# A planner inside a transformer kernel gets other estimates for POOL's pow, for each kind of matmul and for visits to half mode

## The chip, the cores and the metric

One Trainium2 chip (trn2); the kernel runs on one core. The time is device time of one execution in microseconds, and of several executions the median. A second, profiled execution gives the trace.

## The reference

Input is x of 256 tokens by 1024, all in float32. Five layers follow one another, each with a residual:

- **layer ab**: RMS norm, a projection to queries, keys and values, a sparse attention whose keys are picked by an index score (top 64 of 256), a forgetting attention beside it (8 heads of 64 each), an output projection
- **mlp**: RMS norm, 1024 to 4096, squared relu, 4096 to 1024
- **layer c**: RMS norm, a projection, an attention of 16 heads in three branches (compressed, selected, window) with gates, an output projection
- **mlp** again, then a last RMS norm
- **layer d**: differential attention, where each of 16 heads has two score maps of 64 columns each whose softmaxes are subtracted

```python
q = rms_norm(q.reshape(b, s, 16, 2, 64), q_norm_g) * 64 ** -0.5
k = rms_norm(k.reshape(b, s, 16, 2, 64), k_norm_g)
scores = einsum('bqhmd,bkhmd->bhmqk', q, k)
probs = softmax(scores + alibi_bias, axis=-1)
weights = probs[:, :, 0] - lam * probs[:, :, 1]
o = rms_norm(einsum('bhqk,bkhe->bqhe', weights, v), head_norm_g) * (1 - lam_0)
out = x + (o.reshape(b, s, 2048) * silu(z)) @ w_out
```

## The kernel before

**Staging.** All weights come from HBM once, in loads of 512 KB that one generator (`fetch`) issues in a fixed sequence on SP's queue. Each load is split into a high part, rounded to float32r (`round_off`, on ACT or VectorE), and a remainder (`remainder`, on VectorE). A product is a **triple** of matmuls into one PSUM bank (`mm3`): high by high, high by low, low by high. The 256 tokens are two tiles t = 0, 1 of 128. `proj` runs eight k-steps of such triples for both tiles into two banks and hands each finished bank to an evacuation; `out_proj` does the same for the four output banks. The two MLPs are the longest stretches: seven chunks, each with 96 matmuls of 256 columns (up) and 48 of 512 (down), after a first one.

**The order is made by a planner.** Nothing in the kernel's text fixes the order of instructions. Every stage is a generator, a strand, that yields one operation at a time or a wait for an event, a buffer or a time. `_Weaver.run` (line 217) simulates the engines: T is TensorE, A ACT, D VectorE, P POOL, Q SP's queue. At each step it takes the strand that can start first (ties by priority, then by age), emits its operation, and moves the engine's clock on by the operation's cost. `LAT` (line 157) is added where an operation's input comes from another engine. Where a strand offers a list of operations, one per engine, the one that ends first in the plan is taken. What is emitted is the program: each engine runs its instructions in exactly that order, and on the chip semaphores make it wait wherever an operand isn't there.

So an estimate does nothing to an instruction's own time. It decides what stands ahead of it on its engine. The costs come from two places: `_Engine.cost` (line 116) for ACT, VectorE and POOL, and `T` (line 325) for TensorE. The planner also keeps a count of TensorE's work for its clock (`clock`, line 180): where the count is low, it takes TensorE's costs double.

**POOL's pow.** A reciprocal square root is a `tensor_tensor` with `pow` and a constant of -0.5 on POOL (`rsqrt`, line 519), on one column (a row's norm), four (`drn`) or eight (`qrs`).

**The turn from one head group to the next in layer d.** `group` (line 1661) runs four projections per group (q, k, v, z), then spawns four heads whose attention is woven into the next group's projections. The evacuation of q and of k is `qk_ev` (line 1640): Square on ACT, a reduction `qss` on VectorE, a scalar step, the pow `qrs` on POOL, a scaling `n` on VectorE, then `transp4` (line 660): four transposes on TensorE and a copy back.

```python
yield act.activation(out=sq, in_=ps, func=AF.Square)
te = yield dve.tensor_reduce(out=ss, in_=heads(sq), axis=AX.X, op=ALU.add)
yield dve.tensor_scalar(out=ss, in0=ss, scalar1=rq[t], scalar2=EPS, op0=ALU.mult, op1=ALU.add)
rs = yield from rsqrt(ss, 8, "qrs")
te = yield dve.scalar_tensor_tensor(out=heads(q), in0=heads(ps), scalar=r[t], in1=rs..., op0=ALU.mult, op1=ALU.mult)
yield from transp4(q, dst[:, :, t * P:(t + 1) * P], gp, evs[t])
```

**Half mode.** Scores of heads of 64 columns are done two heads at a time (`scores2`, line 680): the operands of one head lie on partitions 0 to 63, of the other on 64 to 127, so each matmul uses half of the array's rows, and two run beside one another. One such operation, four float32 matmuls (recorded as eight), is a **visit**. They occur in the index of layer ab, in its two attentions, and in the heads of layer d.

**Ropes.** `rope_on` (line 633) rotates the first 16 columns of each head with four POOL operations: three products into `T` and one sum into `n`; a rope over eight heads has the widths 128, 64, 64 and 128.

The line of almost every operation in the trace is 113 (ACT, VectorE, POOL), 341 (matmuls) or 339 (transposes): these are the helpers that emit it. So rows are told apart by tiles: `wH` and `wL` are a weight's high part and remainder, `slot` the big buffers, `n` the 512-column buffers, `uH` and `uL` a layer's input, `E` a score map.

Of the kernel before, what the change touches and what calls it, by code (L numbers as in the profile page):

```python
# [10 lines left out]
F32 = mybir.dt.float32  # L11
F32R = mybir.dt.float32r
# [73 lines left out]
class _Op:  # L86
# [4 lines left out]
    def __init__(self, eng, cost, emit, bank=None, work=0.0):  # L91
        self.eng, self.cost, self.emit, self.bank, self.work = eng, cost, emit, bank, work


def _free(ap):
    n = 1
    for x in ap.shape[1:]:
        n *= x
    return n


class _Engine:
# [13 lines left out]
    def cost(self, name, a, kw):  # L116
        out = kw.get("out", a[0] if a else None)
        src = kw.get("in_", kw.get("in0", a[1] if len(a) > 1 and hasattr(a[1], "shape") else out))
        n = _free(out)
        if name in ("tensor_reduce", "max"):  # L120
            n = _free(src)
        ptr = sum(hasattr(kw.get(k), "shape") for k in ("scale", "bias", "scalar", "scalar1", "scalar2"))
        ps = src.space == PSUM
        if self.key == "A":
            return 1e-3 * (n / 1.2 + (52 if ps else 93) + 93 * (ptr + ("accum_out" in kw)))
        if self.key == "D":
            if name == "reciprocal":
                return 1e-3 * (69 + 6.25 * n)
            fast = name in ("tensor_copy", "tensor_scalar") and not ps
            return 1e-3 * (69 + n * (0.521 if fast else 1.042) + 62 * ptr)  # L130
        if name == "dma_start":
            return 1.04
        if kw.get("op") == ALU.pow:
            return 1e-3 * (300 + 165 * n)
        if name == "tensor_scalar":
            return 1e-3 * (260 + 3.35 * n)
        return 1e-3 * (147 + (3.1 if name == "tensor_copy" else 2.11) * n)
# [124 lines left out]
def tile_kernel(ctx: ExitStack, tc: tile.TileContext, I: dict, out: bass.AP):  # L262
# [23 lines left out]
    X0 = 2  # L286
    GAINW = 5.5
    HALF = 0
    T1W = 0
    LATE = 7  # L290
    OWN = 8
# [33 lines left out]
    def T(calls, beside=1):  # L325
        late = calls if callable(calls) else lambda: calls
        cost = work = 0.0
        for c in late():
            if len(c) == 3:
                cost += 0.109  # L330
                work += 0.053
            else:
                work += _free(c[0]) * (4 if c[1].dtype == F32 else 1) * c[1].shape[0] / 128 * 0.4167e-3
                cost += 0.003 + (4 * max(_free(c[0]), 128) if c[1].dtype == F32 else max(_free(c[0]), 256 if c[1].dtype == F32R else 128)) * 0.4167e-3

        def emit():
            for c in late():
                if len(c) == 3:
                    i = pe.transpose(c[0], c[1], ident[:c[2], :c[2]])  # L339
                else:  # L340
                    i = pe.matmul(c[0], lhsT=c[1], rhs=c[2], start=c[3], stop=c[4], skip_group_check=True)  # L341
            return i
        return _Op("T", cost / beside, emit, None, work)

    def events(n, m):
        return [[_Event() for _ in range(m)] for _ in range(n)]
# [123 lines left out]
    def setup():  # L470
        def across(dst, src):
            return pool.dma_start(out=dst, in_=src.partition_broadcast(P))

        yield pool.dma_start(out=grow[0:2, :], in_=I["a_kv_norm"][0].rearrange("(k p) -> k p", p=P))
        yield across(kidx_b, I["a_kidx_norm"][0])
        yield across(bforget_b, I["ab_b_forget"][0])
        early.set(W.end + 4.0)
        yield pool.dma_start(out=grow[2:18, :], in_=I["mlp_norm"].rearrange("l (k p) -> (l k) p", p=P))
        for r0, src in ((18, I["final_norm"]), (26, I["l0_norm_g_2"]), (34, I["l0_head_norm_g_2"])):
            n = src.shape[0] // P  # L480
            yield pool.dma_start(out=grow[r0:r0 + n, :], in_=src.rearrange("(k p) -> k p", p=P))
        for r0, src in ((35, I["l0_q_norm_g_2"]), (36, I["l0_k_norm_g_2"])):
            for j in range(2):
                yield pool.dma_start(out=grow[r0:r0 + 1, 64 * j:64 * j + 64], in_=src.rearrange("(k p) -> k p", k=1))
        yield ("at", W.end + GAINW)
        yield ("acq", "B")
        b = bank()
        yield T([tr(b[:, :NG], grow, NG)])
        te = yield dve.tensor_copy(gcol, b[:, :NG])
        W.give("B", te)  # L490
        gain.set(te + 0.2)
        yield dve.tensor_tensor(out=gfd, in0=gcol[:, G_F:G_F + 8], in1=gcol[:, G_D:G_D + 8], op=ALU.mult)
        yield across(bgate_b, I["c_b_gate"][0])


    def warm():
        yield ("acq", "B")
        b = bank()
        while W.now < WARM:
            yield T([mm(b[:, :256], warmth[:, :P], warmth, True, True)])  # L500
        W.give("B", W.end)

    def first_gain():
        yield ("at", 3.2)
        yield ("acq", "B")
        b = bank()
        yield T([tr(b[:, :NA], growA, NA)])
        te = yield dve.tensor_copy(gcolA, b[:, :NA])
        W.give("B", te)
        gainA.set(te + 0.1)  # L510
# [40 lines left out]
    def start_layer(gap, gev, hev, after, first=4, late=None):  # L551
        uev = [[_Event() for _ in range(8)] for _ in range(2)]
        for t in range(2):
            n = first if t == 0 else 4
            for k in range(0, 8, n):
                W.spawn(u_strand(t, k, n, gap, gev, hev, uev[t][k:k + n], late), t + 0.1 * k)
            W.spawn(after(t), 1.5)
        return uev
# [39 lines left out]
    def out_proj(lds, opnd, ev, finish, last=4, halves=False):  # L598
        nk = len(lds)
        pieces = [(t, c * 512, 512) for t in range(2) for c in range(2)]  # L600
        if halves:
            pieces[3:] = [(1, 512, S), (1, 512 + S, S)]
        yield ("acq", "B", len(pieces))
        acc = [bank()[:, :n] for _, _, n in pieces]

        def step(k, i):
            ld = lds[k]
            t, a, n = pieces[i]
            yield ("ev", ld.ready)
            yield ("ev", ev(k))  # L610
            lH, lL = opnd(k, t)
            w = slice(a, a + n)
            yield T(mm3(acc[i], lH, lL, ld.H[:, w], ld.L[:, w], k == 0, k == nk - 1))
            if i != 3 or not halves:
                ld.took()

        for k in range(nk - last):
            for i in range(len(pieces)):
                yield from step(k, i)
        for i, (t, a, n) in enumerate(pieces):  # L620
            for k in range(nk - last, nk):
                yield from step(k, i)
            W.spawn(finish(t, a // 512, acc[i], slice(a, a + n)), 0, W.end + 0.2)
# [292 lines left out]
    def norm_after(hin, r, rev, late=None):  # L916
        def after(t):
            for c in range(2):
                yield ("ev", hin[t][c])
            if late is not None:  # L920
                yield ("ev", late)
            ms = yield from mean_sq(h[:, t, :], D, "ms")
            r[t] = yield from rsqrt(ms, 1, "r")
            rev[t].set(W.end + 0.1)
        return after

    def layer_ab(pl, hin, hout):
        r, rev = [None, None], [_Event(), _Event()]
        aqiw = pl["aqi"]["ld"][LATE].ready
        uev = start_layer(gcolA[:, 0:8], gainA, hin, norm_after(hin, r, rev, aqiw), 2,  # L930
                          pl["aqi"]["ld"][T1W].rounded)
        yield None
# [637 lines left out]
    def layer_d(pl, hin):  # L1570
# [229 lines left out]

        yield from out_proj(pl["out"], opnd, lambda k: oev[k], fin, halves=bool(HALF))

# [52 lines left out]
```

## Time and profile before

| what | value |
| --- | --- |
| median of 3 runs | 924.11 us (922.16 to 925.39) |
| the profiled execution | 921.53 us |
| its span, first to last instruction | 919.4 us |
| mean granted TensorE clock | 0.998 |
| instructions | 14126 |
| TensorE matmuls | 5196 |
| VectorE, ACT, POOL busy | 586.6, 518.2, 106.4 us |
| DMA | 144.55 MB, mean 157 GB/s |

Times in the rows are microseconds from the span's start, unless a column says nanoseconds. A matmul's record lasts longer than its share, since matmuls overlap: what one costs is the distance from its start to the next start. `[0.71 <-DVE n L113]` means that the engine sat idle 0.71 us until VectorE had written n.

### The profile page before, as it was taken

How to read it: one execution, taken by the hardware profiler on the slowest of the kernel's cores; microseconds unless marked ns; L12 is line 12 of the kernel's file. 1: busy time of each engine (PE TensorE's matmuls, PEld its weight loads, DVE VectorE, ACT ScalarE, POOL GpSimd, SP SyncE). 2: the span in 40 equal slices, each digit the busy share in tenths (PEclk: the TensorE clock that was granted, in tenths of full speed). 3: DMA queues.
4: the chain of work that ended last, by engine and by line, in shares of the span. 5: the costliest groups of instructions: out<-in, count | busy, mean ns of one | idle time of the engine just before them, and what ended most of it. 6: DMA issues, size and time to landing. Idle time of an engine off the chain costs nothing.

```text
span 919.4 us, 14126 instructions
## 1 busy us (share of the span) xinstructions
PE 901.2 (98%) x5196; PEld 766.9 (83%) x5196; DVE 586.6 (64%) x1230; ACT 518.2 (56%) x1025; POOL 106.4 (12%) x149
## 2 busy tenths in 40 slices
PE   8999999999999999999999999999999999999998
PEld 6778888999999878888789999998877778777786
DVE  5688646544454457766654445444878878697781
ACT  5666858455544564787575544455637545274450
POOL 3520000000000051120000000000310503204000
PEclk9999999999999999999999999999999999999999
DMA  7756134655555474312236665655674545544431
GB/s 233 207 178 211 55 104 164 203 183 187 189 191 190 133 249 143 110 46 70 74 123 196 208 192 179 198 184 161 161 220 130 159 138 160 165 133 159 140 115 46
DMA packets 65124, 144.55 MB, mean 157 GB/s; under 512 B 7214, under 2 KB 9744, under 8 KB 65056
## 3 DMA queue, kind: packets, MB, share of 16 engines
q1 hardware_dynamic: 63632, 140.68, 48.0%
q0 software_dynamic: 1424, 2.98, 1.6%
q8 instruction: 41, 0.67, 0.3%
q14 instruction: 27, 0.22, 0.1%
HBM read 142.59 MB, written 1.05 MB: 156 GB/s over the span
## 4 chain that ended last, share of the span: by engine, by line
PE 86%; DVE 4%; POOL 4%; DMA 3%; ACT 1%; issue 1%; SPq 0%; POOLq 0%; DVEq 0%; ACTq 0%
PE bank L341 81%; PE bank L339 5%; POOL qrs L113 2%; DVE wL L113 2%; DVE n L113 1%; DMA h<-in_x_dram 1%; ACT wH L113 1%; DMA raw<-in_c_w_in_dram 1%; POOL T L113 1%; POOL drn L113 1%; DMA raw<-in_ab_w_in_dram 1%; DVE qss L113 0%; DMA raw<-in_l_w_in_dram 0%; ACT n L113 0%; DVE dss L113 0%
## 5 line engine op out<-in xcount | busy, mean ns | idle before, releaser
L113 DVE TENSOR_TENSOR wL<-raw,wH 128x1024 fp32r<-128x1024 f32 (+2 forms) x262 | 317.8, 1214 | 187.9 <-ACT wH L113 186.2
L113 ACT CAST wH<-raw 128x1024 fp32r<-128x1024 f32 (+2 forms) x226 | 234.8, 1041 | 225.4 <-PE bank L341 181.4
L341 PE MATMUL bank<-wH,slot 128*128 128x512 f32 (+1 forms) x784 | 258.3, 396 | 1.2 <-ACT slot L113 0.6
L341 PE MATMUL bank<-wH,uH 128*128 128x512 f32 (+2 forms) x448 | 182.8, 408 | 0.5 <-ACT uH L113 0.5
L341 PE MATMUL bank<-wH,uL 128*128 128x512 f32 (+2 forms) x448 | 174.9, 390 | 0.0
L341 PE MATMUL bank<-wL,uH 128*128 128x512 f32 (+2 forms) x448 | 174.6, 390 | 0.0
L341 PEld LDWEIGHTS bank<-wH,slot 128*128 128x128 f32 x784 | 147.2, 188 | 32.1 <-issue 1.7
L341 PE MATMUL bank<-wL,slot 128*128 128x512 f32 (+1 forms) x392 | 152.7, 390 | 0.0
L341 PE MATMUL bank<-uH,wL 128*128 128x256 f32 x448 | 127.4, 284 | 0.0
L341 PE MATMUL bank<-uL,wH 128*128 128x256 f32 x448 | 127.0, 284 | 0.0
L341 PE MATMUL bank<-uH,wH 128*128 128x256 f32 x448 | 126.1, 281 | 0.0
L341 PEld LDWEIGHTS bank<-wH,uH 128*128 128x128 f32 x448 | 85.1, 190 | 20.2 <-issue 2.3
L341 PEld LDWEIGHTS bank<-wH,uL 128*128 128x128 f32 x448 | 84.8, 189 | 18.7 <-DVE uL L113 0.4
L341 PEld LDWEIGHTS bank<-wL,uH 128*128 128x128 f32 x448 | 85.2, 190 | 15.0 <-DVE wL L113 0.2
L341 PEld LDWEIGHTS bank<-uH,wH 128*128 128x128 f32 x448 | 85.0, 190 | 0.6
L341 PEld LDWEIGHTS bank<-uL,wH 128*128 128x128 f32 x448 | 84.3, 188 | 0.6
L341 PEld LDWEIGHTS bank<-wL,slot 128*128 128x128 f32 x392 | 73.8, 188 | 13.0
L341 PEld LDWEIGHTS bank<-uH,wL 128*128 128x128 f32 x448 | 84.6, 189 | 0.0
L113 ACT ACTIVATE E<-E,nb 128x128 f32<-128x128 f32 (+1 forms) x160 | 70.8, 447 | 9.7 <-DVE nb L113 9.6
L113 POOL TENSOR_TENSOR qrs<-qss,neghalf 128x8 f32<-128x8 f32 x16 | 36.3, 2272 | 141.6 <-DVE dss L113 110.0
L341 PEld LDWEIGHTS bank<-slot,PT 128*128 128x128 f32 x384 | 48.7, 191 | 3.9 <-issue 0.7
L113 POOL TENSOR_TENSOR r<-ms,neghalf 128x1 f32<-128x1 f32 x6 | 4.0, 668 | 403.3 <-DVE ms L113 403.3
(206 smaller groups left out, 953.4 us busy)
## 6 DMA issues: line engine op xcount, KB each, us to landing
raw<-in_mlp_w_dram SPq DMA_DIRECT2D x128, 512.0 KB, 3.9
raw<-in_l_w_in_dram SPq DMA_DIRECT2D x64, 512.0 KB, 3.8
raw<-in_ab_w_in_dram SPq DMA_DIRECT2D x16, 512.0 KB, 4.1
raw<-in_l_w_out_dram SPq DMA_DIRECT2D x16, 512.0 KB, 3.4
raw<-in_c_w_in_dram SPq DMA_DIRECT2D x12, 512.0 KB, 4.0
raw<-in_ab_w_out_dram SPq DMA_DIRECT2D x8, 512.0 KB, 3.4
raw<-in_c_w_out_dram SPq DMA_DIRECT2D x8, 512.0 KB, 3.5
slot<-in_ab_w_in_dram SPq DMA_DIRECT2D x8, 256.0 KB, 6.2
```

The costliest lines, as they stand in the source:

```text
L113: return _Op(self.key, self.cost(name, a, kw), lambda: f(*a, **kw), bank[0] if bank else None)
L339: i = pe.transpose(c[0], c[1], ident[:c[2], :c[2]])
L341: i = pe.matmul(c[0], lhsT=c[1], rhs=c[2], start=c[3], stop=c[4], skip_group_check=True)
```

## The change

Four edits in the planner's estimates, none in an operation. In `_Engine.cost`, pow on n columns of POOL costs 0.380 us and 0.175 us a column below eight columns, 0.380 and 0.262 a column from eight on; before it was 0.300 and 0.165 a column. In `T`, a float32r matmul costs 0.0145 us and 0.4167 ns a column (at least 0.112), before 0.003 and the same a column (at least 256 columns). A float32 matmul costs twice 0.004 us and two columns' time a column (at least twice 0.112), before 0.003 and four columns' time (at least 128 columns). Other types keep their formula, with the least cost written as a time. The transposes' cost stays. A T operation that has a matmul on 64 partitions, or with 64 stationary columns, costs 0.4 us more (`SWITCH`), after its sum is divided by the number that run beside one another. The count of work for the clock stays as it was.

```diff
         if kw.get("op") == ALU.pow:
-            return 1e-3 * (300 + 165 * n)
+            return 1e-3 * (380 + (175 if n < 8 else 262) * n)
...
     HALF = 0
+    SWITCH = 0.4
...
         cost = work = 0.0
+        mode = False
         for c in late():
             if len(c) == 3:
                 cost += 0.109
                 work += 0.053
+                continue
+            n = _free(c[0])
+            work += n * (4 if c[1].dtype == F32 else 1) * c[1].shape[0] / 128 * 0.4167e-3
+            mode = mode or c[1].shape[0] == 64 or _free(c[1]) == 64
+            if c[1].dtype == F32:
+                cost += 2 * max(0.112, 0.004 + 2 * n * 0.4167e-3)
+            elif c[1].dtype == F32R:
+                cost += max(0.112, 0.0145 + n * 0.4167e-3)
             else:
-                work += _free(c[0]) * (4 if c[1].dtype == F32 else 1) * c[1].shape[0] / 128 * 0.4167e-3
-                cost += 0.003 + (4 * max(_free(c[0]), 128) if c[1].dtype == F32 else max(_free(c[0]), 256 if c[1].dtype == F32R else 128)) * 0.4167e-3
+                cost += max(0.056, 0.003 + n * 0.4167e-3)
+        cost = cost / beside + (SWITCH if mode else 0.0)
...
-        return _Op("T", cost / beside, emit, None, work)
+        return _Op("T", cost, emit, None, work)
```

## Rows read from the trace of the kernel before

**Rows 1.** The page, busy time of each engine (share of the span) and its instructions.
```profile
PE 901.2 (98%) x5196; PEld 766.9 (83%) x5196; DVE 586.6 (64%) x1230; ACT 518.2 (56%) x1025; POOL 106.4 (12%) x149
```
**Rows 2.** Busy time by stage: stage, length, each engine, clock, DMA share, GB/s.
```profile
317.00:350.00 33.00, 31.12 (x166) 26.89 (x165) 19.38 (x38) 22.56 (x48) 13.35 (x28) 0.95 0.68 212
...
424.00:465.00 41.00, 37.37 (x231) 30.38 (x229) 26.05 (x92) 26.34 (x83) 2.20 (x3) 1.00 0.19 66
...
713.00:736.00 23.00, 22.08 (x112) 17.86 (x112) 18.06 (x38) 11.50 (x16) 12.13 (x6) 1.00 0.53 156
```
**Rows 3.** The chain of waits: start, length, what; the second MLP and a turn.
```profile
479.16 158.87 PE bank L341 x1008
...
727.08 2.49 POOL qrs L113
...
730.62 2.49 POOL qrs L113
```
**Rows 4.** TensorE in order of time around one visit to half mode in layer d.
```profile
695.66 0.40 PE L341 MATMUL bank<-wH,uL 128*128 128x512 f32 x1
695.99 0.93 PE L341 MATMUL bank<-slot 64*128 64x128 f32 x8
696.84 0.50 PE L341 MATMUL bank<-wH,uH 128*128 128x512 f32 x1
697.18 0.39 PE L341 MATMUL bank<-wL,uH 128*128 128x512 f32 x1
```
**Rows 5.** POOL in order of time: a pow of one column, one of eight.
```profile
327.76 0.56 POOL L113 TENSOR_TENSOR r<-ms,neghalf 128x1 f32<-128x1 f32 x1 [3.64 <-DVE ms L113]
...
717.18 1.63 POOL L113 TENSOR_TENSOR qrs<-qss,neghalf 128x8 f32<-128x8 f32 x1
```
**Rows 6.** TensorE in order of time: the first group's transposes, and the first turn.
```profile
675.80 0.40 PE L341 MATMUL bank<-wH,uL 128*128 128x512 f32 x1
676.49 0.66 PE L339 MATMUL bank<-const,n 128*128 128x128 f32 x4 [0.29 <-DVE n L113]
...
720.54 1.03 PE L339 MATMUL bank<-const,n 128*128 128x128 f32 x8
...
724.55 0.48 PE L341 MATMUL bank<-wH,uH 128*128 128x512 f32 x1
...
729.29 0.40 PE L341 MATMUL bank<-wH,uL 128*128 128x512 f32 x1
730.40 0.66 PE L339 MATMUL bank<-const,n 128*128 128x128 f32 x4 [0.71 <-DVE n L113]
...
733.44 0.39 PE L341 MATMUL bank<-wH,uL 128*128 128x512 f32 x1
734.03 0.63 PE L339 MATMUL bank<-const,n 128*128 128x128 f32 x4 [0.21 <-DVE n L113]
```
**Rows 7.** VectorE in order of time: three scalings n at the first turn.
```profile
719.68 0.74 DVE L113 SCALAR_TENSOR_TENSOR n<-bank,rr,qrs 128x512 f32<-128x512 f32 x1
...
729.59 0.75 DVE L113 SCALAR_TENSOR_TENSOR n<-bank,rr,qrs 128x512 f32<-128x512 f32 x1 [0.94 <-POOL qrs L113]
...
733.13 0.75 DVE L113 SCALAR_TENSOR_TENSOR n<-bank,rr,qrs 128x512 f32<-128x512 f32 x1 [1.53 <-POOL qrs L113]
```
**Rows 8.** The chain of waits at layer C's start and at its end.
```profile
335.16 6.54 DMA raw<-in_c_w_in_dram
...
457.10 1.23 DVE wL L113
```
**Rows 9.** POOL's groups by line and shape: count, busy us, mean ns, idle before.
```profile
L113 POOL TENSOR_TENSOR T<-n,const 128x64 f32<-128x64 f32 x16 | 7.4, 481 | 0.0
L113 POOL TENSOR_TENSOR n<-T,T 128x128 f32<-128x128 f32 x8 | 5.6, 696 | 0.5
...
L113 POOL TENSOR_TENSOR T<-n,const 128x128 f32<-128x128 f32 x8 | 4.1, 515 | 24.5 <-ACT n L113 22.2 <-PE bank L341 2.2
```
**Rows 10.** TensorE's waits: for what, us in total, times, longest.
```profile
PE bank L339 <- POOL n L113: 0.7, 1, 0.7
```

## The prediction

> **What bounds the kernel now.** I read the page first: TensorE is busy for 98% of a 919.4 us span, and the next engine for 64% [rows 1]. The reader is to see that only TensorE time counts, and that an edit which adds and removes no instruction can win only what TensorE loses between instructions. Where that is stands in the busy time by stage [rows 2]: layer C's start has 31.12 of 33.00 with a granted clock of 0.95, its end 37.37 of 41.00, and in the last layer a turn from one head group to the next has 22.08 of 23.00; there are three turns, alike. The chain of waits [rows 3] says what a turn waits for: a pow of 2.49 us on POOL and then a second one of 2.49. Its piece of 1008 matmuls, in an MLP, gives the true price of a stretch with nothing to win, 158.87 us.
>
> **The estimates against the rows.** The change edits only what the planner believes, so each belief is set beside its row.
>
> Matmuls: those 1008 are seven chunks with 96 of 256 columns (672) and 48 of 512 (336) each. By the old formula (0.003 us plus 0.4167 ns a column) they cost 672 x 0.1097 + 336 x 0.2163 = 146.4 us, by the new one (0.0145 us plus the same) 672 x 0.1212 + 336 x 0.2278 = 158.0. The chip took 158.87 [rows 3]. So the old plan has TensorE 8.5% too fast, the new one 0.6%. A triple of 512 columns (the planner's unit) goes from 0.649 to 0.683; the chip's is 0.70 (successive starts 0.23 apart, [rows 4]). The Trainium skill, page "TensorE: Matmul & The Clock Gate", section "Back-to-back issue gap", gives N / 2.4 + 2.5 ns, 216 ns at 512 columns. By that rule the old figure is right and the new one 5% too long; dependents would come later in the plan than they need, the lost slack below would be nil, and the sum would be -3.6 instead of -3.1 us. The trace disagrees with the rule: 0.23 us [rows 4].
>
> Visits to half mode: the last triple ahead of a visit begins its third matmul at 695.66, so the visit can begin at 695.89; the next matmul starts at 696.84 and takes 0.34 to its successor instead of 0.23 [rows 4]. That is 0.95 + 0.11 = 1.06 us. The planner had (2 x 0.2163 + 2 x 0.4297) / 2 = 0.646, and will have (2 x 0.224 + 2 x 0.4347) / 2 + 0.4 = 1.059. By the code there are 28 visits (four of the index, four in each of the two attentions of the first layer, 16 in the last), so 28 x 0.41 = 11.6 us of TensorE time become known to the plan. The visits themselves get no cheaper: 0, and nothing hides them.
>
> Pow: eight columns go from 1.620 to 2.476, four from 0.960 to 1.080, one from 0.465 to 0.555. The rows have 2.49 [rows 3] and 1.63 [rows 5] for eight, and 0.56 for one [rows 5].
>
> **What moves, and the sum.** At a turn the planner's chain from a projection's last matmul to the transposes of its result is 0.2 + Square 0.479 + 0.13 + reduction 0.602 + 0.127 + scalar step 0.135 + 0.155 + pow 1.620 + 0.06 + scaling 0.664 + 0.2 = 4.37 us, or 6.7 triples of 0.649, so seven are laid ahead of the transposes. The trace has exactly these seven (21 matmuls from 724.55), and TensorE then waits: its last matmul starts at 729.29 and the transposes at 730.40, 1.11 later where 0.23 would do, a loss of 0.88 us; at the second pair 733.44 to 734.03, a loss of 0.36 [rows 6]. The other two turns repeat both losses, and the first group has one of 0.46 at 675.80 [rows 6]. With the new figures the chain is 5.23 us, or 7.65 triples of 0.683: eight. One more triple is 0.70 us of TensorE work inside the 0.88. The second pair lies behind two pows, so it moves by 1.7 us in the plan, over two triples, and its 0.36 goes whole. Gain: 3 x (0.70 + 0.36) + 0.46 = **3.6 us**; of 0.88, 0.18 stays, because VectorE's weight remainders stand in the chain too. Late next is VectorE, where the scaling is queued among them: it starts at 729.59 only, after 0.94 us of waiting for POOL [rows 7]. The triples that move forward need their weights then; these are in hand, since TensorE goes on after the transposes without a wait for weights [rows 6].
>
> Lost slack: TensorE used to run 1.077 times the plan's length (0.70 / 0.649), which gave every other engine 7% more time than it had asked for; now it is 1.02. A chain of 4.37 us loses 5.5%, or 0.24 us. Where TensorE now arrives later than that after its operand, nothing is lost. The joint nearest is the transposes at 720.54 [rows 6], whose operand's scaling runs from 719.68 for 0.74 [rows 7]: 0.12 of slack. It comes three times, 3 x 0.12 = 0.36, and with what I take for the unread joints **+0.5 us** (an estimate; the ends are 0, if every other joint has more slack than 0.24 and this one is laid later too, and +7.2, worked out with the rival below; I stay near the low end because the nearest joint read gives 0.36).
>
> Layer C's start and end, the long waits, are set at 0: the start waits for a transfer of 6.54 us, which no estimate here changes, and the end for a weight's remainder of 1.23 us on VectorE [rows 8], whose estimate stays. The ends for them: the 3.6 us of idle at the end gone, or a further cold stretch of the size of the one at the start (a mean clock of 0.95 over 33 us means some time at 1.2 GHz instead of 2.4, and 0.05 x 33 = 1.7 us of full-speed work lost). No DMA issue is moved past another on SP's queue: the fetch is one sequence. POOL's DMAs (setup, layer C's small weights, the last gain) can change places with pows and ropes only where both are ready, and lie in stretches where I see no wait for POOL beyond those counted; 0, and if the cover goes, about one pow of 0.56.
>
> The sum against the profiled execution: 921.53 - 3.6 + 0.5 = 918.4 us. That execution was 2.6 us under the median of 924.11; the same 3.1 off the median gives **921.0 us**. A measurement of this kernel can tell 0.3%, 2.8 us, from no change; the forecast lies just beyond that.
>
> **Rivals.**
> *Slower: the ropes show.* POOL's other estimates stay short. A rope over eight heads is planned at 0.417 + 2 x 0.282 + 0.417 = 1.40 us and takes 0.515 + 2 x 0.481 + 0.696 = 2.17 by the rows' means [rows 9], 0.77 longer; there are eight of them, in the first and third layer. The 7% by which the chip's TensorE falls behind the plan hid most of that: TensorE waits for POOL's n only once, 0.7 us [rows 10]. With that gone, up to 8 x 0.77 - 0.7 = 5.5, and 8 x 0.22 (5.5% of a 4 us chain) = 1.7, come out as waits: +7.2, less the 3.6 of the turns, +3.6: 927.7 us. It decides once more than 6.4 us of it show. For: the one rope wait there is. Against: seven of eight have none.
> *Same: the wait changes hands.* In the room that a longer pow leaves, the planner lays another remainder of 1.23 us [rows 8] on VectorE ahead of the scaling. Then the scaling is late by that, TensorE's transposes wait as long as before, and only the second pairs gain: 3 x 0.36 = 1.1 less 0.5, or 923.5 us. For: VectorE is busy 18.06 of 23.00 at a turn [rows 2]. Against: it idles 0.94 and 1.53 us there just for POOL [rows 7].
> *More: layer C as well.* With TensorE's pace true, roundings come in time at layer C's end, and no cold stretch falls at its start: 3.6 + 1.7 on top of the 3.6, 8.9 in all, or 915.2 us. For: TensorE waits there for roundings laid by a planner that has it 8% too fast. Against: nothing in the change touches what is believed of roundings and remainders.
> That nothing is reordered can't be, since every matmul's estimate moves.
>
> **How the numbers follow.** Forecast 0.40 (918.5 to 923, of which 0.25 below the 921.3 that counts as faster and 0.15 above), more 0.22, same 0.16, slower 0.22. Faster 0.25 + 0.22 = 0.47; same 0.15 + 0.16 = 0.31; slower 0.22. The range goes from just under the better case to just over the rope case, 914.5 to 928.0 us; the forecast's own is 918.5 to 923. An order laid by such a planner moves everywhere at once, and that keeps the tails.
>
> **What would show it.** Right: at the turns no TensorE wait over 0.3 us ahead of the transposes, eight triples and not seven between them, the dense pieces still at 158.9 us for 1008 matmuls, the same 28 visits at 1.06. Wrong: waits for POOL's n in the first and third layer over 2 us together (the ropes), a scaling at a turn that stands behind one remainder more (changed hands), or a cold stretch more than the one.

## The result, and the profile after

The changed kernel takes 929.31 us (median of six, 926.43 to 931.58), the kernel before beside it 924.49 (six, 921.05 to 925.39). The ratio is 1.0059 with an interval of 1.0034 to 1.0083: slower by 0.6%, where the forecast had 921.0 us and a range up to 928.0. The profiled execution took 931.58 us, the slowest of its six; the one of before, at 921.53, was 3.0 us under its median. So the two traces are 10.0 us apart where the medians are 4.8, and what follows explains the traces.

The page's span and busy time:

```profile
span 929.8 us, 14160 instructions
PE 911.8 (98%) x5196; PEld 774.8 (83%) x5196; DVE 592.0 (64%) x1240; ACT 511.5 (55%) x1014; POOL 109.7 (12%) x150
```

The number of matmuls is the one of [rows 1], and TensorE is still busy for 98%. So ten more microseconds of span are ten more of busy TensorE: either more expensive instructions, or a slower clock. The share of busy time can't tell the two apart; a table by stage can.

The chain of waits has one long piece of dense matmuls in each MLP, which serves as a ruler. First column: its start, second: its length. The two pieces of the changed kernel:

```profile
159.87 159.60 PE bank L351 x1014
489.36 159.60 PE bank L351 x1014
```

and the first piece of the kernel before (its second is in [rows 3]):

```profile
158.25 158.90 PE bank L341 x1008
```

The changed kernel's pieces hold six matmuls more, which take 0.7 us. From the ends of these pieces, with 479.16 - 0.73 = 478.43 as the start of the second one before:

| stretch | before | after | difference |
| --- | --- | --- | --- |
| up to the end of the first MLP | 317.15 | 319.47 | +2.3 |
| layer C | 161.3 | 169.9 | **+8.6** |
| second MLP | 159.6 | 159.6 | 0 |
| last layer | 281.4 | 280.8 | -0.6 |

Most of the loss is in layer C; the 2.3 us ahead of it come up again under the ropes. The windows of layer C show what its loss is. Columns as in [rows 2]: stretch, length, busy time of PE, PEld, DVE, ACT and POOL with their instructions, then the granted clock as a share of 2.4 GHz, the DMA share and GB/s. The kernel before:

```profile
317.00:375.00 58.00, 56.05 (x312) 48.13 (x311) 35.79 (x78) 34.11 (x69) 19.92 (x46) 0.97 0.58 183
345.50:348.90 3.40, 3.40 (x15) 3.37 (x15) 2.80 (x12) 1.92 (x5) 0.00 (x0) 0.50 0.83 264
348.90:375.00 26.10, 26.02 (x157) 22.34 (x157) 17.50 (x42) 11.87 (x22) 6.57 (x18) 1.00 0.43 142
```

The changed kernel:

```profile
317.00:375.00 58.00, 54.72 (x267) 47.48 (x266) 29.42 (x67) 27.22 (x60) 16.08 (x38) 0.82 0.48 153
347.20:350.60 3.40, 3.21 (x13) 3.25 (x14) 3.40 (x9) 2.24 (x6) 0.00 (x0) 0.50 0.62 169
350.60:357.40 6.80, 6.25 (x48) 5.60 (x47) 5.22 (x14) 4.52 (x11) 2.86 (x10) 1.00 0.62 217
357.40:374.50 17.10, 17.10 (x64) 15.42 (x64) 5.23 (x21) 1.56 (x4) 0.00 (x0) 0.50 0.11 37
```

The first row of each fence already gives the size: a mean clock of 0.82 in place of 0.97 over 58 us is 0.15 x 58 = 8.7 us of full-speed work lost. Both kernels have a short stretch at 1.2 GHz, 3.40 us long, about where a wait of TensorE for duplicated keys ends (1.8 us before, 2.7 after). The changed kernel has a second one, 17.10 us long, in which TensorE is busy all the time and works at half speed: 17.10 x 0.5 = **8.55 us**. That is the 8.6 of the table.

What runs there is the compression of layer C (`cmp_strand`): for each of two strands (y = 0 and 1) 16 float32 matmuls of 30 columns, planned as four blocks of four, which the trace shows as eight records each (`n,slot`). Between the blocks the planner leaves a strand a pause of 1.3 us (`REST`), which it fills with other work. TensorE's timeline of the kernel before (start, length, what it is, count), the blocks and what stands between them:

```profile
349.05 0.97 PE L341 MATMUL bank<-n,slot 128*128 128x30 f32 x8
349.86 0.42 PE L339 MATMUL bank<-const,dup 128*128 128x128 f32 x2
350.12 0.97 PE L341 MATMUL bank<-n,slot 128*128 128x30 f32 x8
...
351.44 0.97 PE L341 MATMUL bank<-n,slot 128*128 128x30 f32 x8
...
352.75 0.97 PE L341 MATMUL bank<-n,slot 128*128 128x30 f32 x8
...
354.56 1.87 PE L341 MATMUL bank<-n,slot 128*128 128x30 f32 x16
...
357.60 1.86 PE L341 MATMUL bank<-n,slot 128*128 128x30 f32 x16
```

and of the changed kernel:

```profile
353.16 1.87 PE L351 MATMUL bank<-n,slot 128*128 128x30 f32 x16
354.86 0.48 PE L351 MATMUL bank<-wH,uH 128*128 128x512 f32 x1
355.18 0.39 PE L351 MATMUL bank<-wL,uH 128*128 128x512 f32 x1
355.41 0.40 PE L351 MATMUL bank<-wH,uL 128*128 128x512 f32 x1
356.31 0.69 PE L349 MATMUL bank<-const,dup 128*128 128x128 f32 x2 [0.50 <-DVE dup L113]
356.84 2.93 PE L351 MATMUL bank<-n,slot 128*128 128x30 f32 x16
...
361.33 3.45 PE L351 MATMUL bank<-n,slot 128*128 128x30 f32 x16
```

Two things differ. Before, the first four blocks stand one by one and the last four in two pairs; after, the two strands run in step and all eight stand in pairs, with one triple between. And one of the transposes of duplicated keys (`const,dup`) that lie among the blocks in both kernels now comes ahead of its operand, so TensorE waits 0.50 us for it. The clock falls inside the pair that follows: 1.87 us for a pair, then 2.93, then 3.45. The duplicate is late because POOL's rope is. VectorE's row for it in the changed kernel:

```profile
355.94 0.23 DVE L113 COPY dup<-n 128x128 f32<-128x128 f32 x1 [0.79 <-POOL n L113]
```

The waits of TensorE by releaser (us in total, times, longest), changed kernel:

```profile
PE bank L349 <- POOL n L113: 2.9, 4, 1.4
PE bank L349 <- DVE dup L113: 1.5, 2, 1.0
PE bank L349 <- DVE n L113: 1.5, 2, 0.9
```

The wait for POOL's n was 0.7 in [rows 10]. The wait for DVE's n was 3.4 us in eight places before, 3.0 of it in seven places in the last layer (the transposes at the head groups). TensorE's timeline of the changed kernel shows the two waits that are left, both in the first group, and then the transposes of k at the first turn, the ones that waited in [rows 6]:

```profile
670.79 0.66 PE L349 MATMUL bank<-const,n 128*128 128x128 f32 x4 [0.61 <-DVE n L113]
...
689.09 0.33 PE L349 MATMUL bank<-const,n 128*128 128x128 f32 x1 [0.89 <-DVE n L113]
...
737.63 0.39 PE L351 MATMUL bank<-wH,uH 128*128 128x512 f32 x1
...
744.37 0.39 PE L351 MATMUL bank<-wH,uL 128*128 128x512 f32 x1
744.60 0.60 PE L349 MATMUL bank<-const,n 128*128 128x128 f32 x4
...
746.90 0.40 PE L351 MATMUL bank<-wH,uL 128*128 128x512 f32 x1
747.13 0.65 PE L349 MATMUL bank<-const,n 128*128 128x128 f32 x4
```

At the turn k's first transposes begin 0.23 us behind the start of the last matmul, with no wait, against 1.11 before [rows 6], and the second ones at 747.13 have none either; the other two turns are alike. The work among them is laid differently: the two come 2.5 us apart and not 3.6, and ten triples (30 matmuls from 737.63 to 744.37) stand ahead of the first where seven stood.

### The profile page after: what moved, and what is told of

The parts are those of the page before. It is cut to its first block, busy times and chain, and to the rows that moved or that the text cites. A ratio compares the mean times of both kernels' runs of the same rounds, so it can differ in the third digit from the quotient of the medians.

```text
span 929.8 us, 14160 instructions
## 1 busy us (share of the span) xinstructions
PE 911.8 (98%) x5196; PEld 774.8 (83%) x5196; DVE 592.0 (64%) x1240; ACT 511.5 (55%) x1014; POOL 109.7 (12%) x150
## 4 chain that ended last, share of the span: by engine, by line
PE 82%; issue 6%; DMA 5%; POOL 3%; DVE 2%; ACT 2%; SPq 0%; POOLq 0%; ACTq 0%; DVEq 0%
PE bank L351 77%; PE bank L349 5%; DMA raw<-in_ab_w_in_dram 2%; DMA raw<-in_l_w_in_dram 1%; POOL T L113 1%; POOL n L113 1%; DMA h<-in_x_dram 1%; ACT wH L113 1%; DVE wL L113 1%; DMA raw<-in_c_w_in_dram 1%; ACT n L113 1%; DVE n L113 0%; DVE slot L113 0%; POOL rck L113 0%; ACT slot L113 0%
## 5 line engine op out<-in xcount | busy, mean ns | idle before, releaser
L113 ACT CAST wH<-raw 128x1024 fp32r<-128x1024 f32 (+2 forms) x218 | 226.7, 1041 | 240.7 <-PE bank L351 202.0
L351 PE MATMUL bank<-wH,slot 128*128 128x512 f32 (+1 forms) x784 | 255.7, 395 | 0.0
L351 PE MATMUL bank<-wH,uH 128*128 128x512 f32 (+2 forms) x448 | 185.0, 413 | 1.1 <-ACT uH L113 1.1
L351 PE MATMUL bank<-slot,PT 128*128 128x64 f32 (+1 forms) x384 | 51.1, 274 | 0.0
```

The source lines that it names most:

```text
L113: return _Op(self.key, self.cost(name, a, kw), lambda: f(*a, **kw), bank[0] if bank else None)
```

## The experiments

The theory: the new matmul estimates lay the compression blocks in pairs and a late operand among them, and there the clock falls for some 17 us. The rivals: the loss is the ropes' waits and the lost slack; or the pow or the visit estimate does it.

A stretch of 17.1 us at half clock lowers an execution's mean clock by 17.1 x 0.5 / 930 = 0.009. All six executions of the changed kernel have 0.988 to 0.993, the profiled one of before has 0.998. A mean clock of 0.993 or less is counted below as "long stretch". It is a mark and no proof: it says that some 13 us or more of an execution ran at half clock (2 x 0.007 x 926), not that they were one piece. Short stretches of 3.4 us add up in it (the profiled execution of e2 has three, and 0.994), and at 0.993 there is no room for the whole 17.1.

**The estimates one at a time.** The first three runs have one edit of the change each.

e2_pow_only, the kernel before with the new pow alone:

```diff
         if kw.get("op") == ALU.pow:
-            return 1e-3 * (300 + 165 * n)
+            return 1e-3 * (380 + (175 if n < 8 else 262) * n)
```

> The kernel before with the new estimate for pow alone. Theory: the compression blocks keep their order of before, so one short stretch at the lower clock as before, and the turns in layer D lose their waits: 924.5 - 3.6 = 920.9 us. Rival (the wait at a turn changes hands): 923.5 to 924.5 us.

Measured 920.73 us, ratio 0.9959 (0.9942 to 0.9976): faster than both kernels. The waits at the head groups are gone; the one for DVE's n that is left lies in layer C:

```profile
PE bank L339 <- DVE n L113: 0.3, 1, 0.3
```

The second MLP's piece in its chain of waits gives the length of its last layer:

```profile
483.03 158.86 PE bank L341 x1008
```

It ends at 641.89, and the span is 919.7: 277.8 us against 281.4 before, 3.6 less, which is the term of the prediction for the turns.

e4_switch_only, the kernel before with the 0.4 us for a visit alone (`SWITCH`).

> The kernel before with the 0.4 us for visits to half mode alone. Theory: the visits take what they took, the compression blocks keep their order; no change, 923 to 926 us. Rival (the longer visits reorder layer D and the first layer for the worse and are part of the loss): 927 us or more.

Measured 922.87 us, 0.9977 (0.9960 to 0.9995), no execution with a long stretch.

e3_mm_only, the changed kernel with the old pow and `SWITCH = 0.0`, so the matmul estimates alone.

> The kernel before with the new estimates for matmuls alone (old pow, visits at 0 extra). Theory: this part alone lays the compression blocks in pairs, so the long stretch at the lower clock comes (about 17 us, 8 to 9 us lost), and the turns keep their waits: 924.5 + 9 = 933 us. Rival (the loss comes from the parts together, or from waits): no long cold stretch here, 924 to 928 us.

Measured 932.42 us, 1.0080 (1.0058 to 1.0102), with the long stretch in four executions of four. Its window in the profile:

```profile
353.00:370.10 17.10, 17.10 (x64) 15.45 (x64) 6.04 (x25) 1.69 (x5) 0.00 (x0) 0.50 0.15 41
```

So the matmul estimates bring it, and neither of the others. e7_pow_switch has both of the others:

```diff
+                mode = mode or c[1].shape[0] == 64 or _free(c[1]) == 64
...
-        return _Op("T", cost / beside, emit, None, work)
+        return _Op("T", cost / beside + (SWITCH if mode else 0.0), emit, None, work)
```

> The kernel before with the new estimates for pow and for visits, the old ones for matmuls. Theory: the two gains add, since the compression blocks keep their order of before: 924.0 - 3.3 - 1.2 = 919.5 us. Rival (both reorder the same turns, and their gains are one and the same): 920.7 us or more.

Measured 923.56 us, 0.9990 (0.9971 to 1.0009), no long stretch. The rival is right here: the gains of pow and visit don't add. Each alone is faster, both together can't be told from the kernel before.

**Is it the clock?** e1_fill gives TensorE work that nothing needs. Behind each of the eight blocks stand three bfloat16 matmuls of zeros into another part of the bank, and the planner isn't told:

```diff
+        def filled(emit, b):
+            def both():
+                emit()
+                for _ in range(FILL):
+                    i = pe.matmul(b[:, 256:512], lhsT=warmth[:, :P], rhs=warmth, start=False, stop=True,
+                                  skip_group_check=True)
...
+                op.emit = filled(op.emit, b)
```

> The changed kernel in its own order on every engine, with three bfloat16 matmuls of 256 columns on zeros added behind each of the eight blocks of compression matmuls in layer C; the planner does not know of them. Theory (the loss is TensorE's clock: 17 us at the lower clock from 357 to 374 us, which costs about half of that): the clock stays at 1.00 there, 929.3 - 8.5 + 24 x 0.11 = 923.4 us, at most 925. Rival (the loss is in waits for other engines, above all for POOL's ropes, now that TensorE's lead is priced in): the added work comes on top, 929.3 + 2.6 = 931.9 us, whatever the clock says.

Measured 923.89 us against 924.03, ratio 1.0007 (0.9984 to 1.0031): 24 matmuls more, and 5.4 us less than the changed kernel's median (not measured again beside it). The window of the compression in the profile has its full clock:

```profile
349.40:375.00 25.60, 25.55 (x172) 22.39 (x171) 15.22 (x44) 10.26 (x20) 3.90 (x14) 1.00 0.41 126
```

One execution of ten still had the long stretch (932.96 us at 0.989). The filler also makes TensorE later, and in this profile no wait for a duplicate is left among the blocks. So e1 shows that the clock was the loss, but not whether the filling or the missing wait kept it up. e11_before_fill is the control, the same filler in the kernel before.

> The kernel before, with the three added matmuls behind each compression block, a control for the filled changed kernel. Theory (the filling costs its 24 x 0.11 us and buys only clock, of which the kernel before has lost little): 924 + 2.6 less at most the 1.7 us of its one short cold stretch, 925 to 926.6 us. Rival (the filling helps in another way, and the filled changed kernel shows that and not the clock): 922 us or less.

Measured 925.53 us, 1.0011 (0.9996 to 1.0026), no long stretch in ten. The filler gains nothing there; the 1.5 us that it costs by the medians aren't clear of the noise. In the changed kernel it takes 24 x 0.11 = 2.6 us of TensorE, so that kernel without the filler and without the stretch would be at 923.9 - 2.6 = 921.3 us, an estimate; with the control's 1.5 us it would be 922.4.

**Is it the pairs?** e5_after_two halves the blocks of the changed kernel, which also doubles the pauses:

```diff
-            for j0 in range(0, 16, 4):
+            for j0 in range(0, 16, 2):
...
-                              for j in range(j0, j0 + 4)])
+                              for j in range(j0, j0 + 2)])
```

> The changed kernel, with the compression matmuls of layer C in blocks of two instead of four, each block with the same rest after it, so that two triples stand between blocks; nothing is added. Theory (clock): no long stretch at the lower clock, and without the 2.6 us of added matmuls of the filled kernel: 929.3 - 8.5 = 920.8 us, between 919 and 922.5. Rival (the order around the blocks costs by its waits and not by the clock): 926 us or more.

Measured 925.99 us, 1.0013 (0.9999 to 1.0028), no long stretch in twelve, although TensorE waits for the duplicate as long as in the changed kernel:

```profile
355.77 0.69 PE L349 MATMUL bank<-const,dup 128*128 128x128 f32 x2 [0.54 <-DVE dup L113]
```

So a wait of half a microsecond isn't enough by itself. The rival is partly right on the time: the doubled pauses push work to layer C's end, where TensorE waits. Between 425 and 476 us it is busy 48.23 of 51.00 in this kernel, and 49.73 in e12 below. That is 1.5 of the 4.3 us by which it lies above e12's executions without the stretch (921.70).

e8_mm_two has the same smaller blocks in e3_mm_only.

> The kernel before with the new estimates for matmuls alone, and the compression blocks of two as in the changed kernel with blocks of two. It weighs what the matmul estimates cost or bring beside the clock. Theory (the prediction's lost slack of 0.5 us): 932.4 - 8 = 924.4 us, at most 925.5. Rival (lost slack is large: waits for POOL's ropes and for VectorE show): 926.5 us or more.

Measured 929.07 us, 1.0058 (1.0035 to 1.0081), one long stretch in ten, although TensorE waits for the duplicate among the blocks even longer:

```profile
353.42 0.68 PE L349 MATMUL bank<-const,dup 128*128 128x128 f32 x2 [1.45 <-DVE dup L113]
```

The 5 us aren't all the matmul estimates': e5 has the same smaller blocks and is 4.3 us above e12. What the estimates themselves cost shows in the last layer, which no edit of the blocks touches. The second MLP's piece of e3 and then of e8:

```profile
485.12 159.60 PE bank L351 x1014
482.78 159.62 PE bank L351 x1014
```

From there to the end of the span (931.1 and 929.4 us) it is 286.4 us in e3 and 287.0 in e8, against 281.4 before; e8 has a short stretch at half clock in it, worth 1.7. The waits for DVE's n, here of e8, are part of it:

```profile
PE bank L349 <- DVE n L113: 5.4, 8, 2.2
```

5.2 us of them lie in the last layer (5.6 in e3), where the kernel before has 3.0; the rest of the 5 us wasn't traced. With TensorE's pace true and pow still short, the plan leaves its other engines too little time. That is the lost slack, and with the new pow estimate most of its waits are gone (1.5 us in two in the changed kernel).

e6_before_rest0 goes the other way and takes the pause out of the kernel before, so that its blocks can stand closer:

```diff
-    REST = 1.3
+    REST = 0.0
```

> The kernel before, old estimates, with the rest after a compression block at 0, so that 28 of the 32 compression matmuls stand together with no triple between. Theory (clock): TensorE goes to the lower clock for 10 us or more from there, although every estimate is the old one: 924 + 5 to 924 + 9, 929 to 933 us. Rival (matmuls moved together cost what they cost; the loss needs the new estimates): 923 to 926 us.

Measured 926.95 us, 1.0030 (1.0010 to 1.0050). That is between the two forecasts, in the direction of the theory: the profile, of one of the three slowest executions, has a stretch at half clock, but of 10.3 us:

```profile
354.00:364.30 10.30, 10.30 (x45) 10.01 (x45) 3.84 (x21) 2.21 (x7) 0.90 (x4) 0.50 0.17 56
```

By the mark of 0.993 six of its ten executions count, and the other four have 0.994. The mark is loose here: the profiled execution's 0.991 is this stretch and two short ones. What the trace adds is that no wait stands among the blocks. Six of the eight follow each other in one piece, and the clock falls inside it, with TensorE busy:

```profile
351.34 7.83 PE L341 MATMUL bank<-n,slot 128*128 128x30 f32 x48
```

e10_before_paired makes pairs in the kernel before, with all its old estimates, by holding one strand 0.9 us back until the other is beside it:

```diff
+            if y == 0:
+                yield ("at", W.now + 0.9)
             for j0 in range(0, 16, 4):
```

> The kernel before, all estimates old, with the first compression strand starting 0.9 us later in the plan, which lays the blocks in pairs with one triple between, as the changed kernel has them. Theory: the long stretch at the lower clock comes without any new estimate, 10 us of it or more, and the time is 924 + 5 to 924 + 8 = 929 to 932 us. Rival (the pairs alone don't do it): 923 to 926 us.

Measured 930.74 us, 1.0072 (1.0054 to 1.0089), the long stretch in six of six. The trace has the same picture, a wait among the blocks and then half clock:

```profile
354.41 0.68 PE L339 MATMUL bank<-const,dup 128*128 128x128 f32 x2 [0.57 <-DVE dup L113]
```

```profile
355.10:372.10 17.00, 17.00 (x62) 15.06 (x62) 5.56 (x21) 1.92 (x4) 0.00 (x0) 0.50 0.22 62
```

One line of delay in the old kernel brings the changed kernel's loss, with none of its estimates: the order is what costs. This execution had no short stretch ahead of the compression either (its matmuls at 347 us run at full speed), so the long one doesn't need a preceding one.

**The pairs or the wait?** e9_after_apart holds one strand of the changed kernel back, to set the two apart again:

```diff
+            if y == 1:
+                yield ("at", W.now + 1.45)
             for j0 in range(0, 16, 4):
```

> The changed kernel, with the second of the two compression strands starting 1.45 us later in the plan. Against the changed kernel only TensorE's order within the compression moves (the first blocks stand alone between triples, then pairs); nothing is added, and the other engines keep their order but for a few lines. Theory (the pairs bring the long stretch at the lower clock, and that is the loss): the long stretch goes or shrinks to a short one like that of before, and the time is that of the filled kernel less its filling, 923.9 - 2.6 = 921.3 us, between 920 and 923. Rival (the order as a whole is worse, and the clock is a part of it only): 926 us or more, as for the blocks of two.

Measured 930.76 us, 1.0070 (1.0045 to 1.0095), six of six with the long stretch: a miss. The edit set only the first three blocks apart; from the fourth on they stand in pairs again, now shifted by one. And the wait among them grew to 1.00 us:

```profile
355.25 0.69 PE L349 MATMUL bank<-const,dup 128*128 128x128 f32 x2 [1.00 <-DVE dup L113]
```

So this run says nothing of blocks that stay apart. e12_after_late leaves the pairs and takes the wait, by holding back the transposes of the second keys in `dup_strand`:

```diff
+            if y == 1:
+                yield ("at", W.now + 1.2)
             yield ("acq", "B")
```

> The changed kernel, with the transposes of the second keys' duplicates starting 1.2 us later in the plan. Against the changed kernel each of the two moves half a pair later on TensorE (so the two middle pairs have them in their middle), and five lines move on VectorE. Theory of the wait (TensorE's wait for late duplicates between the blocks sets off the long cold stretch): the wait of 0.5 us is gone, the stretch too, 920 to 923 us. Theory of the density (too little matmul work among the blocks, whatever it waits for): pairs and triples are as many as before, so the stretch stays, 927 us or more.

The transposes now wait for nothing, and the profiled execution keeps its clock:

```profile
354.19 0.41 PE L349 MATMUL bank<-const,dup 128*128 128x128 f32 x2
```

```profile
350.60:374.50 23.90, 23.71 (x142) 20.23 (x142) 15.57 (x43) 10.43 (x21) 7.00 (x18) 1.00 0.45 142
```

But its twelve executions fall into two groups with nothing between:

| executions | mean clock | us | median |
| --- | --- | --- | --- |
| 7 | 0.997 to 0.999 | 920.41 to 923.41 | 921.70 |
| 5 | 0.988 to 0.991 | 930.83 to 931.82 | 931.50 |

The median over all is 923.35, the ratio 1.0012 (0.9981 to 1.0043), which says little of a kernel with two times. The groups say more: one program in one order, 9.8 us apart, and nothing between. The mean clocks of the groups, 0.9983 and 0.9904, account for 7.3 of the 9.8; the rest wasn't traced.

e13_apart_late has both edits, of e9 and of e12.

> The kernel of e9_after_apart (the second compression strand 1.45 us later), with the duplicates' transposes 1.2 us later in the plan as well. It has single blocks at both ends and three pairs between, and should have no wait for duplicates. Theory of the wait: no long cold stretch, 920 to 923 us. Theory of the density: the stretch stays, 928 to 931 us, as in e9_after_apart.

Measured 922.28 us, 0.9982 (0.9963 to 1.0000). Two executions of eleven had the long stretch (928.59 and 929.51), the other nine took 921.4 to 924.1. The profile caught one of the two. The first block stands alone and the others in pairs; the clock falls inside the first pair, at 354.00, ahead of the only wait among the blocks, of 0.18 us:

```profile
352.54 2.15 PE L351 MATMUL bank<-n,slot 128*128 128x30 f32 x16
...
354.87 0.83 PE L349 MATMUL bank<-const,dup 128*128 128x128 f32 x2 [0.18 <-DVE dup L113]
```

```profile
354.00:371.00 17.00, 16.82 (x64) 15.07 (x64) 6.53 (x25) 2.89 (x7) 1.01 (x7) 0.50 0.24 71
```

Put together, by the profile of each kernel, with the number of executions that had the long stretch:

| kernel | blocks | wait for dup among them, us | long stretch |
| --- | --- | --- | --- |
| before (beside the experiments) | four alone, then two pairs | none | 2 of 94 |
| after | four pairs | 0.50 | 6 of 6 |
| e3, matmul estimates | four pairs | 1.29 | 4 of 4 |
| e10, before paired | a pair, two alone, two pairs | 0.57 | 6 of 6 |
| e9, after apart | three alone, then pairs | 1.00 | 6 of 6 |
| e4, visits alone | as before | 0.30, ahead of the last pair | 0 of 10 |
| e6, before without the pause | one alone, six together, one alone | none | 6 of 10 (10.3 us in the profile) |
| e12, after late | pairs, the second and third with transposes inside | none | 5 of 12 |
| e13, apart and late | one alone, then pairs | 0.18, after the fall | 2 of 11 |
| e1, after with filler | pairs, filled | none | 1 of 10 |
| e5, after in blocks of two | pairs, half as long | 0.54 | 0 of 12 |
| e8, matmul estimates in blocks of two | pairs, half as long | 1.45 | 1 of 10 (one short stretch there in the profile) |

The four kernels with blocks of full size and a wait of 0.50 to 1.29 us among them fell every time, blocks in pairs or closer without that wait some of the time, and smaller blocks with the wait once in 22. The counts come from three chips (e1 to e4 and e9 to e11, e5 to e8, e12 and e13), and the changed kernel wasn't run again beside the experiments, so a difference like 5 of 12 against 6 of 6 is weak. What decides in a single execution of e12 or e13 stays open: of each only one was profiled. It also stays open which of the matmul estimates, float32r or float32, brings the strands into step; they were only changed together.

## Why the prediction was wrong, point by point

**The step that failed** is "Layer C's start and end, the long waits, are set at 0". The start cost 8.55 us. The prediction had a second fall among its bounds, "a further cold stretch of the size of the one at the start", and priced it at 1.7 us from the only one the trace had, 3.40 us long. The new one is five times as long. The error has two parts. I looked at layer C for late operands only, not at which of TensorE's instructions stand there; the profile of before showed a clock that falls in this place, and blocks that a strand's pauses keep apart, and an edit to every matmul's estimate moves just those. And I took the length of one stretch as the size of any. It was 3.4 us at layer C's start, but 10.3 in e6 and 17.1 here, where the compression itself ran in it; what sets the length was not tested.

**The rest of the sum holds, though not by its terms.** Without the stretch the changed kernel is at 921.3 us (e1 less its filler) or 921.7 (e12's upper group), that is 2.7 and 2.9 us under the kernel before of the same runs (924.03 and 924.64). The forecast was 3.1 under. Both figures flatter it: with the control's cost of the filler e1 is 1.6 under, and against executions of before with as high a mean clock (0.997 or more, median 923.46) e12's group is 1.8 under. That the sum comes so near is luck: the last layer gave 0.6 us of the 3.1, layer C without a cold stretch gave 2.6 that were set at 0, and the stretch up to the first MLP's end took some 2 back.

**Matmul estimates.** The pieces of [rows 3] return at 159.60 us for 1014: the matmuls didn't change, as forecast, and the new formula is within 1% of them.

**Visits.** No gain was given to them, and no visit got cheaper; but knowing of them alone was worth 0.23% (e4), by an interval that ends at 0.05%. That was set at nothing and is a small miss.

**The turns.** The waits went, as forecast, at all three turns, and pow alone gives the whole 3.6 us (e2). The sign named for it, "eight triples and not seven", did not come as such: ten stand there, since the plan laid the turn anew instead of adding one. The pows themselves changed too: the sixteen of eight columns take 2.48 us in the median before, but 1.75 in the changed kernel and 1.66 in e2, so that the new estimate of 2.476, near the longer ones, is long for most of them. In the full change the last layer gains only 0.6 us (over all profiles that have either order there, 281.4 to 282.8 us became 280.4 to 281.1): 3.0 of waits for DVE's n there became 1.5, all of it in the first group, where 0.46 had been counted. The rest of what was given back has no wait in the profile and wasn't traced further.

**Lost slack**, set at +0.5 with an end of 7.2, was mis-sized. With the old pow it makes the last layer 5.0 us longer (e3), 2.6 of it in waits, and with the new one it takes back most of that layer's gain. The nearest joint was misread besides: the eight transposes at 720.54 [rows 6] are two fours, the first of them for finished heads, and those of the scaling at 719.68 begin at 720.97. Its slack was 0.55 us and not 0.12, and it was no guide to the unread joints.

**Ropes.** The rival's waits came: POOL's n from 0.7 to 2.9 us, past the 2 us that the prediction named as its sign, 1.4 of it in the first layer and 1.5 in layer C. Up to the first MLP's end this pair of traces is 2.3 us longer, in part by chance: with one order of the first layer the traces of before, e6, e10 and e11 end there at 317.15 to 319.45, and with the other those of after, e1, e5, e9, e12 and e13 at 318.85 to 321.10, 1.6 apart in the mean. That is short of the 6.4 from which that rival decides. But a rope is also what makes the duplicate late, so it has a part in the 8.55 that the rival didn't foresee.

**More, layer C as well.** It does gain there where the clock stays up. The pieces of e12's profiled execution:

```profile
159.76 159.60 PE bank L351 x1014
478.09 159.60 PE bank L351 x1014
```

Layer C takes 478.09 - 319.36 = 158.7 us (before 161.3); 1.7 of the 2.6 is the short stretch at its start, which that execution lacks. The sign that was named as "wrong", a cold stretch more than the one, is the one that came.

**The wait changes hands** did not happen at the turns in the form described. With pow and visits together (e7) waits are back that pow alone lacks: 1.6 us for DVE's n in the last layer, and 1.8 for POOL's n against 1.1. Whether that is why the two gains don't add is not shown.

## What to carry to other kernels

Where the clock falls once in a profile, look at the instructions around the place and ask what an edit does to their spacing, not only to waits; and price a second fall by the work that would run in it, at half speed, not by the length of the first. Correct a planner's estimates one at a time: here pow alone is the fastest version measured (920.73 us), and the truer estimates of the matmuls took away slack that other engines had used (the last layer of e3 is 5 us longer). Read the mean clock of every execution beside its time, since a median over two clocks describes neither.

## What the runs showed of the hardware

The clock fell although TensorE had been busy 6.25 of the 6.80 us before, with no wait longer than 0.5 us; and it stayed at 1.2 GHz for 17.1 us in which TensorE was busy throughout. What ran was float32 matmuls of 30 columns with single triples between; it rose again at 374.50, after triples alone since 369.29. A page of the Trainium skill, "TensorE: Matmul & The Clock Gate", section "HAM oscillation — how this bites in real kernels", puts falls of the clock in a kernel of its own down to waits for data between bursts of matmuls. The run with the wait taken out agrees in part (5 of 12 instead of 6 of 6), and e5, with the wait and without the fall, shows that here it isn't the wait alone. In e6 the clock fell after 7.0 us in which TensorE was busy throughout (347.0 to 354.0). So what the engine does between waits counts too; what exactly, stays open. And the same program (e12) on the same chip took 921.7 or 931.5 us, with a mean clock of 0.9983 or 0.9904.
